# A Gated DeltaNet and chunk attention trunk: new planned durations, two yields, and the ends of the FFNs in another order

## The chip, the core and the metric

The kernel runs on one core of one Trainium2 chip. A core has five instruction queues, each in order: PE (TensorE, matmuls and transposes, with PEld as its weight load), DVE (VectorE), ACT (ScalarE), POOL (GpSimd) and SP (SyncE, which only issues DMAs). The engines meet through semaphores; data lies in SBUF (128 partitions) and PSUM (where matmuls add up). The metric is device microseconds (us) of one execution.

## What is computed

The input is a sequence of 1024 rows of width 1024 in float32. Layer 0 is a gated DeltaNet (8 heads of 128, chunks of 64) and a convolutional FFN of width 2816; layer 1 is softmax attention over bands of chunks and such an FFN; a last RMSNorm follows.

```python
def gated_deltanet(xn, w_in, conv_w, A_log, dt_bias, out_norm_w, w_out):
    proj = xn @ w_in
    qkv = jax.nn.silu(causal_dwconv(proj[..., :A_CONV_WIDTH], conv_w))
    z = proj[..., A_CONV_WIDTH:A_CONV_WIDTH + A_V_WIDTH]
    ...
    o = chunk_gated_delta_rule(q, k, v, beta, g)
    o = rmsnorm(o, out_norm_w) * jax.nn.silu(z.reshape(bsz, seq, A_HEADS, A_HEAD_V))
    return o.reshape(bsz, seq, A_V_WIDTH) @ w_out

# in chunk_gated_delta_rule, for each chunk of 64 rows
    v_new = u_c - w_c @ state
    o_c = qd @ state + a_c @ v_new
    state = state * dec + ke.T @ v_new

def conv_ffn(xn, w_up, conv_w, conv_b, w_down):
    h = causal_dwconv(xn @ w_up, conv_w) + conv_b
    gate, val = h[..., :FFN_DIM], h[..., FFN_DIM:]
    return (jax.nn.silu(gate) * val) @ w_down

def trunk(h):                       # the loop over layers, written out
    h = h + gated_deltanet(rmsnorm(h, a_norm[0]), ...)
    h = h + conv_ffn(rmsnorm(h, f_norm[0]), ...)
    h = h + chunk_attention(rmsnorm(h, b_norm[0]), ..., kv)
    h = h + conv_ffn(rmsnorm(h, f_norm[1]), ...)
    return rmsnorm(h, final_norm)
```

## The kernel before

**Precision.** Each float32 operand of a matmul is split into a high and a low part of a shorter type: ACT casts the high part (`whi` of a weight, L102; `uh`, `eh`, `dh`, L1444; `fh`, L1854), and POOL or DVE subtracts it from the original for the low part (`wlo`, L104; `ul`, `el`, `fl`, all on the helper line L1423). A product is then three matmuls (high by high, high by low, low by high). A moving operand has 512 columns.

**Stages.** The trace shows, in order: the prologue (norm of x and its transposes, until about 60 us), the delta stage (60 to 680), the first FFN (until about 1300), attention and the second FFN (its last stretch from 2455 on), and the last norm. In the delta stage the projections, the delta rule and the out projection are woven together.

**The delta stage's planner.** The order of PE, DVE and ACT is written by `Flow` (from L199): it keeps a planned time `T`, a planned "free from" time for D (DVE), A (ACT) and G (POOL), and a list of jobs (Python generators) with ranks. `wv.on("D", cost)` books `cost` us on an engine and returns when it is done; `yield t` gives the turn back until planned time `t`; `later` does so for a function. Between the jobs PE gets dense matmuls (of a projection's or the out projection's weight tile). Costs change no instruction, only which one is issued next. POOL and SP take their instructions in an order that the framework's scheduler sets. Two lines carry the planner's core:

```python
self.free[e] = max(self.free[e], self.T + 0.2, after if e != "G" else 0.0) + cost + 0.05
return max(self.free[e], after + cost) + 0.1
```

Its jobs that the change touches:

- `split_tile` (L639) splits a weight tile of a projection: a cast on ACT, four pieces on POOL (L104).
- `project` (L667) does the short convolution on DVE (L682, L686) and SiLU by tanh (ACT L691, POOL L692 and L693); its `th` is one of a pair of 512-column buffers with the tag `zt`, which `yo`, `zt`, `ez` and `sq` share.
- `qnorm` (L716) transposes (PE L721) and takes sums of squares (ACT L725). `decay` (L750) makes the decay matrices. `gram` (L738) makes k k^T, scales it on DVE into `mn` (L790), and copies the diagonal blocks on POOL into `cm` (L795).
- `invert_blocks` (L851) inverts the 32x32 diagonal blocks on DVE column by column; `merge` (L890, PE L911 to L952) builds larger inverses from them.
- `chain` (L978) is the recurrence over chunks: PE L992 (w by state), DVE L994, PE L996 (`U`), ACT `y` L1001, PE L1005, and DVE L1011, which updates the state S.
- `finish` (L1019) normalises outputs: squares on ACT, an inverse square root by integer tricks and Newton steps on tiny DVE tiles (`rsqrt`, L607 to L612, into `rr`), and a scaling of `vv` on POOL (L1041). Then `turn` (L1047, PE L1051, into PSUM `po`) for all but the last heads, whose results go to DRAM and come back in `yz` (L1105) with their gates, or `turn_last` (L1091, PE L1098). `split_yt` (L1122) splits the result for the out projection, whose tiles (`out_tile`, L1306, PE `acco`) go over the first half of the sequence (s = 0) and then over the second (s = 1).
- `begin_input` (L1225) loads the first two weight tiles and x, and runs transposes and the first products.

`gg`, which holds log decays, is read for the last time by the cumulative sums in the prologue (L1206).

**The FFN.** Width 2816 is 22 tiles j of 128 channels. The up product of a tile (gate and value, 2 x 1024 columns) is computed by a Strassen scheme of seven products, in the order 1, 7, 6, 5, 2, 4, 3; each is 12 matmuls into a PSUM bank. Products 2, 4 and 3 add into the banks of 1, 7 and 5. After product 6 the tile's `keep` and `keep7` are made on DVE from the banks of 6 and 7 (two operations named `keep`, L1423), after 5, 4 and 3 the other parts of the result (`vpre`, `gpre`). `left_sum(j, n)` prepares the weight sum r of product n on DVE; `operand(j, n)` splits it. The convolution is three taps each (`taps`, DVE L1551, ACT L1548), then `silu` (ACT L1554), `gated` (DVE, val x gate) and, for the last four tiles (18 to 21), `hidden` (ACT `hidh` L1568, DVE `hidl`). The others go through nine groups of Strassen down products, whose sums stand in DRAM: `send` and `send_e` add stages by accumulating DMAs that POOL issues (L1793, L1800). Tiles 18 to 21 are multiplied plainly in the end phase "f": `cut_last` (L1851) splits their down weights, and `part` (L1865, first FFN) or `tile_of` (L1939, second) run the matmuls for k = 0 to 3, one k a tile. Until now a first sweep over the column (or row) tiles takes k = 0 to 2, a second k = 3, for the first half; the other half has all four at once.

The order is by hand: `step` appends a PE step to a list `seq`, `pos` holds its place, and `at(i, f, rank)` puts other engines' work ahead of step i, by rank. `end` is the place of the last up product, `fin_at` that of the last down group's product 4.

**The last norm.** `norm_out` (L2325): ACT's Square with a sum (the last tile in two halves), a square root, DVE's reciprocal (L2347), then for each half a DVE operation with the scale and the gain `g_fin` (L2349) and a store on SP's queue (L2350).

## Time and profile before

| what | value |
|---|---|
| runs (3) | median 2588.57 us, 2588.05 to 2591.74 |
| the profiled execution, its own time | 2588.85 us |
| its span, first to last instruction | 2587.0 us |
| granted TensorE clock over the span | 0.996 |
| PE busy | 2506.2 us, 97% |
| DVE, POOL, ACT busy | 1861.0, 1476.3, 1414.3 us |
| DMA packets | 325.15 MB, mean 126 GB/s |

How to read the lines that follow. A timeline row has the start and the length in us, the engine, the line of the kernel, the operation, output<-inputs, partitions x elements and type, and how many instructions were joined (x2); in brackets stands how long the engine was idle before it, and what ended that. A row of waits has the engine, what it wanted to run, what released it, the total us, the number of waits and the longest. A row of groups has the count, busy us, mean ns of one, and the idle time before them. A row of windows has the window, its length, the busy us and count of PE, PEld, DVE, ACT and POOL, PE's granted clock as a share of full speed, the DMA engines' busy share and GB/s. PE's matmuls overlap: a row's 0.39 us is its passage, and the next starts 0.227 us later.

### The profile page before, as it was taken

The numbers are of one execution on the slowest core, as the hardware profiler recorded it, in microseconds if no ns is written. First come the engines' busy times: TensorE is split into PE (matmuls) and PEld (weight loads), VectorE is DVE, ScalarE is ACT, GpSimd is POOL, SyncE is SP. The second block draws the span as 40 slices with busy tenths as digits, with TensorE's granted clock in tenths as the row PEclk, the third lists the DMA queues.
The fourth block names the chain that finished last, engine by engine and source line by source line (L and its number), as shares of the span: only waits on it lengthen the run. The fifth ranks groups of instructions, "written<-read, shape, count | busy, mean of one in ns | idle before, by whom it ended". The sixth has DMA issues, their size and how long they took to land.

```text
span 2587.0 us, 39395 instructions
## 1 busy us (share of the span) xinstructions
PE 2506.2 (97%) x13933; PEld 2068.8 (80%) x13933; DVE 1861.0 (72%) x3102; ACT 1414.3 (55%) x2735; POOL 1476.3 (57%) x1466
## 2 busy tenths in 40 slices
PE   7999999999999999999999999999999999999988
PEld 5878788888877888888788888887876788888877
DVE  5765864554588888888876666666488788888875
ACT  6444455464455555655556555565455655565553
POOL 3655543345437777777726444443433777777770
PEclk9999999999999999999999999999999999999999
DMA  4534435555436777777841211113332576777785
GB/s 128 139 100 118 127 101 161 147 166 156 121 82 135 147 144 153 156 153 152 173 157 54 65 52 56 45 50 100 104 97 79 138 151 143 154 155 150 158 190 174
DMA packets 320598, 325.15 MB, mean 126 GB/s; under 512 B 32912, under 2 KB 244624, under 8 KB 320400
## 3 DMA queue, kind: packets, MB, share of 16 engines
q1 hardware_dynamic: 289584, 219.59, 29.0%
q0 software_dynamic: 25920, 94.38, 20.5%
q10 hardware_dynamic: 4896, 8.65, 1.0%
q8 instruction: 110, 1.80, 0.3%
q14 instruction: 88, 0.72, 0.1%
HBM read 179.89 MB, written 142.67 MB: 125 GB/s over the span
## 4 chain that ended last, share of the span: by engine, by line
PE 54%; DVE 6%; POOL 3%; issue 3%; ACT 2%; DMA 1%; DVEq 0%; ACTq 0%; POOLq 0%
PE pu L1458 8%; PE pu L1456 8%; PE pu L1457 8%; PE pd L1458 4%; PE pd L1457 4%; PE pd L1456 4%; PE acc L119 3%; PE acc L120 3%; PE acc L121 3%; PE ptp L2137 2%; POOL ul L1423 2%; PE sc L2109 1%; PE poT L2167 1%; PE poT L2166 1%; PE sc L2110 1%
## 5 line engine op out<-in xcount | busy, mean ns | idle before, releaser
L1423 POOL TENSOR_TENSOR ul<-r,uh 128x512 fp32r<-128x512 f32 x282 | 445.4, 1598 | 304.9 <-ACT uh L1444 280.9
L119 PE MATMUL acc<-xh,whi 128*128 128x512 f32 x896 | 375.4, 419 | 0.2
L120 PE MATMUL acc<-xl,whi 128*128 128x512 f32 x896 | 354.0, 395 | 2.0 <-POOL xl L421 1.0
L121 PE MATMUL acc<-xh,wlo 128*128 128x512 f32 x896 | 352.7, 394 | 0.0
L1444 ACT CAST uh<-r 128x512 fp32r<-128x512 f32 x296 | 181.7, 623 | 218.0 <-DVE r L1423 176.8
L104 POOL TENSOR_TENSOR wlo<-wraw,whi 128x256 fp32r<-128x256 f32 (+2 forms) x206 | 169.4, 851 | 159.1 <-ACT whi L102 139.3
L1456 PE MATMUL pu<-xh,uh 128*128 128x512 f32 x552 | 216.0, 391 | 2.8 <-ACT uh L1444 1.3
L1458 PE MATMUL pu<-xh,ul 128*128 128x512 f32 x552 | 215.7, 391 | 1.7 <-POOL ul L1423 1.7
L1457 PE MATMUL pu<-xl,uh 128*128 128x512 f32 x552 | 215.5, 390 | 1.0 <-POOL xl L421 1.0
L1778 ACT COPY stage<-pd 128x1024 f32<-128x1024 f32 x180 | 174.8, 1013 | 49.4 <-PE pd L1458 49.4
L121 PEld LDWEIGHTS acc<-xh,wlo 128*128 128x128 f32 x896 | 168.9, 189 | 37.3
L120 PEld LDWEIGHTS acc<-xl,whi 128*128 128x128 f32 x896 | 170.2, 190 | 25.5 <-DVE xl L1163 3.2
L119 PEld LDWEIGHTS acc<-xh,whi 128*128 128x128 f32 x896 | 169.9, 190 | 21.7 <-ACT xh L1162 1.1
L2117 POOL TENSOR_SCALAR sS<-sS,st 128x640 f32<-128x640 f32 (+4 forms) x128 | 85.3, 668 | 172.4 <-DVE st L2116 125.2
L1551 DVE SCALAR_TENSOR_TENSOR val<-vpre,colt,val 128x1023 f32<-128x1023 f32 (+2 forms) x92 | 152.8, 1661 | 38.6 <-ACT val L1548 38.4
L1423 POOL TENSOR_TENSOR dl<-a,dh 128x512 fp32r<-128x512 f32 x90 | 154.7, 1719 | 38.4 <-ACT dh L1444 38.4
L1551 DVE SCALAR_TENSOR_TENSOR gate<-gpre,colt,gate 128x1023 f32<-128x1023 f32 (+2 forms) x92 | 175.1, 1903 | 0.8
L1423 DVE TENSOR_TENSOR r<-r,r 128x512 f32<-128x512 f32 x168 | 131.8, 785 | 31.0 <-POOL ul L1423 29.6
L2115 ACT ACTIVATE sS<-sS,st 128x640 f32<-128x640 f32 (+4 forms) x128 | 89.3, 697 | 101.7 <-DVE st L2114 100.2
L1458 PEld LDWEIGHTS pu<-xh,ul 128*128 128x128 f32 x552 | 103.8, 188 | 26.0 <-POOL ul L1423 4.6
L1456 PEld LDWEIGHTS pu<-xh,uh 128*128 128x128 f32 x552 | 103.9, 188 | 25.3 <-ACT uh L1444 1.8
L1457 PEld LDWEIGHTS pu<-xl,uh 128*128 128x128 f32 x552 | 103.9, 188 | 23.5 <-POOL xl L421 2.1
(401 smaller groups left out, 7158.9 us busy)
## 6 DMA issues: line engine op xcount, KB each, us to landing
r<-in_f_w_up_dram SPq DMA_DIRECT2D x176, 256.0 KB, 4.3
d_r<-stage POOLq DMA_DIRECT2D x78, 512.0 KB, 7.8
d_c<-stage POOLq DMA_DIRECT2D x70, 512.0 KB, 8.1
a<-in_f_w_down_dram SPq DMA_DIRECT2D x72, 256.0 KB, 2.8
wraw<-in_a_w_in_dram SPq DMA_DIRECT2D x32, 512.0 KB, 4.7
d_e<-stage POOLq DMA_DIRECT2D x32, 512.0 KB, 8.9
wraw<-in_a_w_out_dram SPq DMA_DIRECT2D x16, 512.0 KB, 4.0
d_r<-h ACTq DMA_DIRECT2D x32, 256.0 KB, 3.8
```

Source lines behind the costliest of these rows:

```text
L104: nc.gpsimd.tensor_tensor(lo[:, c], raw[:, c], hi[:, c].bitcast(F32), op=ALU.subtract)
L119: mm(ps, hi[:, kw, wcol : wcol + P], rh[k][s], start=st, stop=False)
L120: mm(ps, hi[:, kw, wcol : wcol + P], rl[k][s], start=False, stop=False)
L121: mm(ps, lo[:, kw, wcol : wcol + P], rh[k][s], start=False, stop=sp)
L1423: tt = lambda eng, o, a, b, op: eng.tensor_tensor(o, a, b, op=op)
L1444: copy(hi, src)
L1456: mm(ps, w[0][:, cw], x[0], start=first, stop=False, skip_group_check=True)
L1457: mm(ps, w[0][:, cw], x[1], start=False, stop=False, skip_group_check=True)
L1458: mm(ps, w[1][:, cw], x[0], start=False, stop=last, skip_group_check=True)
L1551: nc.vector.scalar_tensor_tensor(t_[:, a:c1], p_[:, a - step : c1 - step], w[:, 2 - step : 3 - step], t_[:, a:c1], op0=ALU.mult, op1=ALU.add)
L1778: nc.scalar.copy(t_, ps)
L2115: nc.scalar.activation(S, S, AF.Exp, bias=st[:, 1:2], accum_out=st[:, 2:3])
```

## The change

The change has seven parts.

1. Planned durations are changed in `split_tile` (POOL is now booked, with 2.75), `decay`, `gram`, the scale's and `finish`'s rsqrt (1.2 to 3.5, 1.3 to 3.6), the columns of `invert_blocks`, the gate products, `split_yt` and `out_tile`.
2. `gram` yields ahead of POOL's copies into `cm`, and `finish` ahead of POOL's scalings of `vv`, until the DVE work that they read is through by the plan.
3. The tag `zt` has three buffers in the place of two; `soo` takes the place in memory of `gg`.
4. `yz` for the first half gets rank 1.5 in the place of 3.
5. `begin_input` splits the second weight after three steps of transposes.
6. The ends of both FFNs: r of tile 21's product 7 is prepared earlier; the last gate taps, SiLU and product of tile 20 come one step later; `hidden` of tiles 19 and 20 moves to product 5 of tile 21 and to the step after the last; the accumulating DMAs of `send_e` are issued by POOL behind more of its splits; the down weights' splits (`cut_last`) move; and the end phase's first half has three sweeps, with k = 0 and 1, then 2, then 3.
7. In the last norm's last tile the halves are multiplied by the gain ahead of the scale's arrival, and scaled one on DVE and one on ACT, whose queue also issues the second store.

```diff
@@ -612,7 +612,7 @@
-        soo, ff, rr = gt("soo"), gt("ff"), gt("rr")
+        soo, ff, rr = gg, gt("ff"), gt("rr")
@@ -638,7 +638,7 @@
-            wv.on("A", 1.0)
+            wv.on("G", 2.75, wv.on("A", 1.0))
@@ -687,7 +687,7 @@
-                    th = dp.tile([P, HALF], F32, name="th", tag="zt", bufs=2)
+                    th = dp.tile([P, HALF], F32, name="th", tag="zt", bufs=3)
@@ -750,12 +750,12 @@
-                yield wv.on("D", 0.75) - wv.slack
+                yield wv.on("D", 0.8) - wv.slack
...
-                yield wv.on("A", 1.4)
+                yield wv.on("A", 1.45)
@@ -785,10 +785,11 @@
-                wv.on("D", 1.4)
+                wv.on("D", 1.95)
...
-                slot[0] = t_ = wv.on("D", 1.3)
+                slot[0] = t_ = wv.on("D", 1.2)
+                yield t_ - wv.slack
@@ -799,7 +800,7 @@
-            wv.mark(("scale", t), wv.on("D", 1.2))
+            wv.mark(("scale", t), wv.on("D", 3.5))
@@ -877,7 +878,7 @@
-                t_ = wv.on("D", 0.3 + 3.1e-3 * i * i)
+                t_ = wv.on("D", 0.4 + 2.2e-3 * i * i)
@@ -1035,7 +1036,8 @@
-            t_ = wv.on("D", 1.3)
+            t_ = wv.on("D", 3.6)
+            yield t_ - wv.slack
@@ -1050,7 +1052,7 @@
-            yo = dp.tile([P, HALF], F32, name="yo", tag="zt", bufs=2)
+            yo = dp.tile([P, HALF], F32, name="yo", tag="zt", bufs=3)
@@ -1114,7 +1116,7 @@
-            yield wv.on("D", 0.7) - wv.slack
+            yield wv.on("D", 0.85) - wv.slack
@@ -1126,11 +1128,11 @@
-            wv.mark(("act", k, s), wv.on(e, 0.7 if e == "D" else 1.3, t))
+            wv.mark(("act", k, s), wv.on(e, 0.95 if e == "D" else 1.35, t))
...
-                zt = dp.tile([P, HALF], F32, name="zt", tag="zt", bufs=2)
+                zt = dp.tile([P, HALF], F32, name="zt", tag="zt", bufs=3)
@@ -1189,7 +1191,7 @@
-            ez = dp.tile([P, HALF], F32, name="ez", tag="zt", bufs=2)[:, 0:136].rearrange("p (c j) -> p c j", j=8)
+            ez = dp.tile([P, HALF], F32, name="ez", tag="zt", bufs=3)[:, 0:136].rearrange("p (c j) -> p c j", j=8)
@@ -1230,7 +1232,8 @@
-            wts = [load_w(a_w_in, m * P) for m in (8, 9)]
+            raws = [raw_tile(m * P) for m in (8, 9)]
+            wts = [split_w(raws[0], [P, KT, P])]
@@ -1240,6 +1243,8 @@
+                if s == 0:
+                    wts.append(split_w(raws[1], [P, KT, P]))
@@ -1274,7 +1279,7 @@
-        env["tmp"] = lambda: dp.tile([P, HALF], F32, name="sq", tag="zt", bufs=2)
+        env["tmp"] = lambda: dp.tile([P, HALF], F32, name="sq", tag="zt", bufs=3)
@@ -1328,7 +1333,7 @@
-                wv.on("D", 0.65, wv.on("A", 0.65))
+                wv.on("D", 0.75, wv.on("A", 0.65))
@@ -1337,7 +1342,7 @@
-            wv.later(wv.on("D", 0.6), then)
+            wv.later(wv.on("D", 0.7), then)
@@ -1385,7 +1390,7 @@
-                wv.add(3, ("yz", n % 6), wv.when(*[("gram", hd, 1) for hd in range(4, 8)]), yz(k, s))
+                wv.add(1.5 if s == 0 else 3, ("yz", n % 6), wv.when(*[("gram", hd, 1) for hd in range(4, 8)]), yz(k, s))
@@ -1648,6 +1653,8 @@
+                if j == FP - 1 and n == 1:
+                    at(i - 2, lambda j=j: left_sum(j, 7), 1.05)
@@ -1690,10 +1697,11 @@
-            when[j] = [(pos[j, 7], (v0, v1), 2), (nx(j, 1), (v2, g0), 2), (nx(j, 2), (g1,), 2)]
-            when[j] += [(nx(j, 3), (g2,), 2), (nx(j, 4), (silu,), 1.6), (nx(j, 5), (gated,), 2)]
+            late_ = 1 if j == FP - 2 else 0
+            when[j] = [(pos[j, 7], (v0, v1), 2), (nx(j, 1), (v2, g0), 2), (nx(j, 2 + late_), (g1,), 2)]
+            when[j] += [(nx(j, 3 + late_), (g2,), 2), (nx(j, 4 + late_), (silu,), 1.6), (nx(j, 5 + late_), (gated,), 2)]
             if j >= 2 * NG:
-                when[j].append(({18: fin_at + 5, 19: fin_at + 7}.get(j, nx(j, 6)), (hidden,), 1.9))
+                when[j].append(({18: fin_at + 5, 19: pos[FP - 1, 5], 20: end + 1}[j], (hidden,), 1.9))
@@ -1821,19 +1829,15 @@
-            for k, n in enumerate((6, 7, 4)):
-                at(i + 2 + k // 2, lambda u=u, n=n: send_e(u, n), 0.6)
+            for n, (k, r) in zip((6, 7, 4), ((2, 0.6), (2, 2.9), (3, 2.9)) if u == 0 else ((2, 2.9), (3, 2.9), (4, 2.9))):
+                at(i + k, lambda u=u, n=n: send_e(u, n), r)
...
-        last_at = [pos[FP - 1, s] for s in (3, 4, 5, 6)] + [end + 1] * 4
-        if layer == 1:
-            last_at = [pos[FP - 1, 2]] + last_at[:-1]
-            last_at[5] = end
-            last_at[7] = end + 2
+        last_at = [pos[FP - 1, s] for s in (3, 4, 5, 6)] + ([end, end, end + 1, end + 1], [end + 1, end + 1, end + 3, end + 3])[layer]
@@ -1858,7 +1862,7 @@
-            at(last_at[q], lambda q=q: cut_last(q), 1.5)
+            at(last_at[q], lambda q=q: cut_last(q), 0.9 if layer == 0 else 1.5)
@@ -1889,10 +1893,9 @@
-            for m in range(KT):
-                step(("f", 0, m, 0), part(0, m, range(3)))
-            for m in range(KT):
-                step(("f", 0, m), part(0, m, range(3, 4)))
+            for i, ks in enumerate((range(2), range(2, 3), range(3, 4))):
+                for m in range(KT):
+                    step(("f", 0, m, i) if i < 2 else ("f", 0, m), part(0, m, ks))
@@ -1975,10 +1978,9 @@
-            for t in range(4):
-                step(("f", t, 0), tile_of(t, range(3)))
-            for t in range(4):
-                step(("f", t), tile_of(t, range(3, 4)))
+            for i, ks in enumerate((range(2), range(2, 3), range(3, 4))):
+                for t in range(4):
+                    step(("f", t, i) if i < 2 else ("f", t), tile_of(t, ks))
@@ -2338,13 +2340,21 @@
+                nc.vector.tensor_tensor(ht[:, 0:HALF], ht[:, 0:HALF], g_fin[0][:, 0:HALF], op=ALU.mult)
                 yield
-                nc.scalar.activation(jk[:, HALF:SEQ], ht[:, HALF:SEQ], AF.Square, accum_out=ss[:, 0:1])
+                nc.vector.tensor_tensor(jk[:, HALF:SEQ], ht[:, HALF:SEQ], g_fin[0][:, HALF:SEQ], op=ALU.mult)
+                nc.scalar.activation(jk[:, 0:HALF], ht[:, HALF:SEQ], AF.Square, accum_out=ss[:, 0:1])
...
+            if t == KT - 1:
+                nc.vector.tensor_scalar(ht[:, 0:HALF], ht[:, 0:HALF], ss[:, 1:2], None, op0=ALU.mult)
+                nc.scalar.activation(ht[:, HALF:SEQ], jk[:, HALF:SEQ], AF.Copy, scale=ss[:, 1:2])
+                for i, q in enumerate((nc.sync, nc.scalar)):
+                    q.dma_start(out=out[t * P : (t + 1) * P, hs(i)], in_=ht[:, hs(i)])
+                return
...

```

## What is predicted, and from what

> **What bounds the kernel now.** I read the page's busy times first, then busy times by stage, then the waits of PE inside the stages that the change reaches, and last the timeline around each wait.
>
> ```profile
> PE 2506.2 (97%) x13933; PEld 2068.8 (80%) x13933; DVE 1861.0 (72%) x3102; ACT 1414.3 (55%) x2735; POOL 1476.3 (57%) x1466
> ...
> 60.00:680.00 620.00, 600.62 (x4918) 504.48 (x4917) 365.86 (x959) 304.20 (x833) 312.80 (x419) 1.00 0.48 137
> 1230.00:1300.00 70.00, 65.54 (x279) 52.81 (x278) 56.85 (x52) 35.89 (x53) 49.21 (x37) 0.98 0.83 185
> 2455.00:2545.00 90.00, 83.36 (x361) 66.52 (x361) 68.74 (x67) 41.95 (x61) 54.59 (x41) 0.96 0.90 220
> ```
>
> PE is busy for 97% of the span: the matmuls set the time, and the change neither adds nor removes one. It can only win or lose idle time of PE, and time in which PE runs at a lowered clock. The three window rows (length, then busy us of PE, PEld, DVE, ACT and POOL, PE's granted clock, share of DMA, GB/s) are the delta stage, and the ends of the first and the second FFN. Idle in them: 620 - 600.62 = 19.4 us, 70 - 65.54 = 4.5 us, 90 - 83.36 = 6.6 us. What the clock costs shows in short windows behind PE's gaps:
>
> ```profile
> 300.00:304.00 4.00, 3.91 (x15) 3.27 (x16) 3.56 (x5) 1.78 (x3) 4.00 (x7) 0.62 0.00 0
> 1289.60:1294.00 4.40, 4.40 (x13) 3.51 (x14) 3.73 (x4) 2.14 (x4) 2.72 (x2) 0.64 0.59 173
> 2520.30:2526.40 6.10, 6.10 (x15) 4.76 (x16) 6.10 (x6) 3.71 (x6) 4.36 (x3) 0.50 0.70 188
> ```
>
> PE is busy in all three at 0.62, 0.64 and 0.50 of its clock, so the work lost is 0.38 x 4.0 = 1.5, 0.36 x 4.4 = 1.6 and 0.50 x 6.1 = 3.05 us. I book these on the gaps just ahead of them.
>
> **The delta stage.** The new durations, the three-buffer tag, the rank of yz and the two new yields (`gram`, `finish`) act together: the planner writes another order of PE, DVE and ACT, and the same instructions run. Their worth is what PE waits for there:
>
> ```profile
> PE pq L721 <- POOL kq L693: 5.0, 3, 2.3
> PE pc L992 <- DVE S L1011: 3.6, 4, 2.3
> PE po L1051 <- POOL vv L1041: 2.5, 1, 2.5
> PE pm L911 <- DVE T L907: 1.8, 2, 1.3
> ...
> POOL vv L1041 <- DVE rr L612: 23.7, 7, 8.7
> ...
> 298.98 2.06 POOL L1041 TENSOR_TENSOR vv<-vv,rr 128x512 f32<-128x512 f32 x2 [8.69 <-DVE rr L612]
> ...
> 300.09 0.65 PE L1051 MATMUL po<-ident,vv 128*128 128x128 f32 x4 [2.54 <-POOL vv L1041]
> ...
> 578.22 1.15 DVE L608 TENSOR_SCALAR rr<-rr 128x8 int32<-128x8 int32 x1
> ...
> 583.00 0.17 DVE L612 SCALAR_TENSOR_TENSOR rr<-t,rr 128x8 f32<-128x8 f32 x1
> ...
> 596.21 2.82 POOL L104 TENSOR_TENSOR wlo<-wraw,whi 128x256 fp32r<-128x256 f32 x4 [2.73 <-ACT whi L102]
> ```
>
> The first four rows hold 5.0 + 3.6 + 2.5 + 1.8 = 12.9 us of the 19.4. The POOL row shows what `finish`'s yield is about: GpSimd stands 23.7 us in front of its scalings, 8.7 us at once, with whatever comes next in its queue (SiLU products, weight splits) behind them. Two rows further, that wait reaches PE: `po` starts 2.54 us late, and this gap is the one ahead of the 0.62 clock. The rsqrt behind it was planned at 1.3 us; from its first row shown to its last it takes 583.17 - 578.22 = 4.95 us here. A weight tile's split was planned at nothing on GpSimd and takes 2.82. With 3.6 and 2.75 the planner sees both, so a turn's transposes and a weight's first matmul stand later in PE's order and find their data ready.
>
> Which stalls vanish can't be read from the order alone, as a new order has new stalls. Bounds: every idle moment and the lowered clock gone, -20.9; idle doubled, +19.4. I take two thirds of the four rows and of the clock, (12.9 + 1.5) x 0.67 = -9.6, and give back 3.6, as much as the four waits on S, for stalls that the new order makes: **-6.0**. The new yields add no wait on an engine; they let the planner place other work ahead of GpSimd's scalings and copies. What stands behind them on GpSimd is then less held up. The turns move back in PE's order: the last one stood some 19 us of matmuls (at the 0.227 us a matmul that the FFN's row times below give) ahead of the out tiles that need it, and now 9; with less than that left over, PE stands at once, as in the 2.54 row.
>
> `soo` in the place of `gg` could add a wait for gg's last reader; that one is in the prologue's cumulative sums (L1206), ahead of every chain and `finish`: nothing. **The first weights** cost nothing either way: ACT still casts both in a row and GpSimd splits all eight pieces in the same place, in the order that the changed kernel is built with. Were the second split to move behind transposes, GpSimd alone would feel it; no matmul of that weight comes sooner.
>
> **The sends ahead of the FFN ends.** One of GpSimd's accumulating DMAs in each FFN (L1800) goes from ahead of operand splits to behind them.
>
> ```profile
> 1234.73 1.53 POOL L1800 DMA_DIRECT2D d_r<-stage  x1
> ...
> 1235.35 2.24 POOL L1423 TENSOR_TENSOR ul<-r,uh 128x512 fp32r<-128x512 f32 x1
> 1235.46 3.93 DVE L1423 TENSOR_TENSOR r<-r,r 128x512 f32<-128x512 f32 x1 [2.09 <-POOL ul L1423]
> ...
> 1239.31 0.68 DVE L1423 TENSOR_TENSOR val<-val 128x512 f32<-128x512 f32 x1
> ...
> 1241.61 0.49 PE L1456 MATMUL pd<-eh,dh 128*128 128x512 f32 x1 [0.86 <-ACT stage L1778]
> ```
>
> DVE's r takes 3.93 us beside GpSimd's splits, where the same operation takes 0.68 alone; ACT's eviction follows late, and PE loses 0.86. Without the send in front, the split starts 1235.35 - 1234.73 = 0.62 us sooner and all of this moves with it: -0.6 in each FFN (the second has the same order), **-1.2** in all, between 0 and -1.7.
>
> **First FFN's end.**
>
> ```profile
> 1283.34 0.39 PE L1456 MATMUL pu<-xh,uh 128*128 128x512 f32 x1
> 1283.59 2.31 DVE L1423 TENSOR_TENSOR hidl<-val,hidh 128x1024 fp32r<-128x1024 f32 x1
> 1285.82 2.29 DVE L1551 SCALAR_TENSOR_TENSOR gate<-gpre,colt,gate 128x1022 f32<-128x1022 f32 x1
> 1285.83 0.39 PE L1458 MATMUL pu<-xh,ul 128*128 128x512 f32 x1
> 1288.03 1.41 DVE L1423 TENSOR_TENSOR keep<-pu,keep 128x512 f32<-128x512 f32 x2
> 1289.58 0.47 PE L1456 MATMUL pu<-xt4h,uh 128*128 128x512 f32 x1 [3.36 <-DVE keep L1423]
> ```
>
> PE waits 3.36 us for the two `keep`s, which read the banks of products 6 and 7; product 4 (xt4h) adds into the latter. Both products were over before product 5, and that before product 2 began (1283.34); the keeps only stand behind hidl of tile 19 and a gate tap, 2.31 + 2.29 = 4.6 us. The change moves both behind them. The keeps then end near 1288.03 + 1.41 - 4.6 = 1284.8, ahead of product 2's end at 1285.83 + 0.23 = 1286.06. Gain 3.4, and 1.6 of clock: **-5.0**, at least -2. Late next are vpre, which frees product 3's bank, and that hidl. With r and gate in front vpre ends by 1284.8 + 0.7 + 2.3 + 0.7 = 1288.5; with fl too, hidl ends by 1288.5 + 1.4 + 2.3 = 1292.2, if GpSimd slows every one. A product takes 12 matmuls, 2.72 us (1283.34 to 1286.06; 0.227 each), so product 3 starts at 1288.8, the end phase at 1291.5, and that needs hidl behind three matmuls of tile 18 and two with hidh, at 1291.5 + 5 x 0.227 = 1292.6. Both just hold. Tile 20 is due only in the new second sweep of the end phase, after 48 matmuls or 10.9 us. The third sweep changes no count of matmuls.
>
> **Second FFN's end.**
>
> ```profile
> 2512.27 0.62 ACT L1444 CAST uh<-r 128x512 fp32r<-128x512 f32 x1 [4.88 <-DMA r<-in_f_w_up_dram]
> 2512.94 0.50 PE L1456 MATMUL pu<-xh,uh 128*128 128x512 f32 x1 [1.34 <-ACT uh L1444]
> 2514.30 0.50 PE L1458 MATMUL pu<-xh,ul 128*128 128x512 f32 x1 [0.62 <-POOL ul L1423]
> 2514.39 2.19 DVE L1423 TENSOR_TENSOR hidl<-val,hidh 128x1024 fp32r<-128x1024 f32 x1 [3.66 <-ACT hidh L1568]
> 2516.50 2.29 DVE L1551 SCALAR_TENSOR_TENSOR gate<-gpre,colt,gate 128x1022 f32<-128x1022 f32 x1
> 2518.72 1.41 DVE L1423 TENSOR_TENSOR keep<-pu,keep 128x512 f32<-128x512 f32 x2
> 2520.27 0.77 PE L1456 MATMUL pu<-xt4h,uh 128*128 128x512 f32 x1 [3.38 <-DVE keep L1423]
> ...
> q0 software_dynamic: 1109, 4.04, 77.3%
> ...
> r<-in_f_w_up_dram SPq DMA_DIRECT2D x1, 256.0 KB, 16.0
> ```
>
> Here 1.34 + 0.62 + 3.38 us are idle and 3.05 go to the clock: 8.4. Keep again stands behind hidl and gate. But a weight load r lands 16.0 us after its issue while GpSimd's queue q0 holds the DMA engines 77.3% of the time (2483 to 2511), and in the new order ACT's cast of a down weight (fh) stands behind the cast of that r, and DVE's fl, another gate and the keeps behind fh. With r as late as now: fh until 2512.9 + 0.6, fl 0.7, gate 1.3, keeps 1.4, so 2516.9 against product 2's end at 2516.7. The gap shrinks from 3.4 to about 0.3 and the clock stays up: -3.1 - 3.05. Of the other 1.96 I take 0.85, as the sends start later and leave q0 open a little, and give 0.5 back for vpre, which with r and gate in front ends at up to 2520.6 where product 3 wants it at 2519.7: **-6.5**, between -3 and -8.4.
>
> **The last scaling.**
>
> ```profile
> 2581.19 0.63 ACT L2342 ACTIVATE jk<-ht 128x512 f32<-128x512 f32 x1 [2.17 <-DVE ht L1423]
> ...
> 2582.47 1.42 DVE L2349 SCALAR_TENSOR_TENSOR ht<-ht,ss,g_fin 128x512 f32<-128x512 f32 x2
> ```
>
> Two halves in a row on DVE, 1.42 us, become one on DVE beside one on ACT, near the Square's 0.63: 0.8 less for the second store, which gets ACT's queue. No store from that queue shows here; I take **-0.7**, between -0.8 and +0.5. The product with g_fin hides beside the Square.
>
> **Sum.** -6.0 - 1.2 - 5.0 - 6.5 - 0.7 = -19.4. The profiled execution took 2588.85 us (span 2587.0), 0.28 above the median of the runs: 2569.45 by its own time, **2569.2** as a median.
>
> **Rivals.** (1) The new order is no better: the waits of the delta stage go to other places. For it: 12.9 us in ten waits are 2% of the stage, any order may have them. The other parts alone give 2588.57 - 13.4 = 2575.2. (2) r comes later still, as q0's sends now reach further, and all of product 2 and the keeps with it: -3 there, 2572.7. Against it: the sends' bytes are the same. (3) The lowered clock isn't the gaps': it comes anyway, elsewhere, and the sum loses its 1.0 + 1.6 + 3.05 = 5.65 us: 2574.8. Against it: all three drops stand right behind a gap. The Trainium skill ("TensorE: Matmul & The Clock Gate", section "What's actually happening") has the clock fall after an idle window of 3413 ns; by that rule these gaps, of 2.54, 3.36 and 3.38 us, are too short to lower it, which is this rival; the trace doesn't agree, with 0.62, 0.64 and 0.50 behind them.
> (4) Slower: the chain.
>
> ```profile
> L1011 DVE SCALAR_TENSOR_TENSOR S<-S,dec,pc 128x128 f32<-128x128 f32 x32 | 11.0, 343 | 17.6 <-PE pc L1005 17.5
> ```
>
> Each of these 32 updates releases PE's next chain step; four are late now, at 3.6 / 4 = 0.9 us. If the new order puts DVE's longer work (4.95 us of rsqrt) ahead of most, the delta stage loses 0.9 for each; the other parts' 13.4 are eaten at 15 late updates, and 0.2% (5.2 us, about what tells a difference from none) is passed at 21. With 30: 2588.57 + 27 - 13.4 = 2602.2. Against it: PE has dense tiles to put between the steps, and the dearer durations space them wider.
>
> **How the numbers follow.** Forecast 0.50, (1) 0.18, (2) 0.10, (3) 0.04, (4) 0.13; 0.05 for 10 to 20 new chain stalls, which end within 0.2%. So faster 0.82, same 0.05, slower 0.13. The forecast's own bounds: all of the four waits and clock gone, the ends at their best, -14.4 - 1.7 - 5.0 - 8.4 - 0.8 = -30.3, 2558; nothing in the delta stage, 2575. The range reaches further down, for part of the other idle time there (up to -20.9, 2552), and up to some 14 late updates: 2555 to 2587.
>
> **What would show it.** Right: no PE wait on keep in either FFN end and clock 1.00 behind; GpSimd's wait on rr far under 23.7; PE idle in the delta stage near 13 us; the last two stores within 0.2 us of each other. Wrong: waits on S, U or turned tiles adding up to more than 19.4 us; r still landing after 2512 relative to the same product; a wait on hidl at the end phase's first tile.

## The result and the profile after

| | before | changed |
|---|---|---|
| first set of runs, median (range) | 2589.47 us (2588.05 to 2591.74, 4 runs) | 2574.11 us (2571.88 to 2575.93, 4 runs) |
| ratio, 95% interval | | 0.9939, 0.9922 to 0.9957 |
| second set, beside other kernels | 2590.74 us (9 runs) | 2570.84 us (5 runs), ratio 0.9924, 0.991 to 0.9939 |
| profiled execution: own time, span | 2588.85, 2587.0 us | 2572.95, 2571.2 us |

The change is a gain of 0.6 to 0.8%. Its forecast was 2569.2 us. As no matmul was added or removed, the span divides at PE's own milestones: the first matmul of each stage. (The changed kernel's lines lie a little lower in the file: L1461 to L1463 are the matmuls of L1456 to L1458, L1428 is the helper line L1423.)

| stretch | before | after | difference | forecast |
|---|---|---|---|---|
| start to the first FFN's first matmul | 679.88 | 667.36 | -12.5 | -6.0 |
| from there to its end phase | 616.83 | 612.71 | -4.1 | -5.6 |
| first FFN's end phase | 46.0 | 53.3 | **+7.3** | 0 |
| attention | 562.1 | 562.2 | +0.1 | 0 |
| second FFN to its end phase | 623.9 | 617.6 | -6.3 | -7.1 |
| to the end of the span | 58.3 | 58.0 | -0.3 | -0.7 |
| span | 2587.0 | 2571.2 | -15.8 | -19.4 |

The timeline rows of the kernel before that bound the first and third stretch (start, length, engine, line, what; the end phase's last matmul closes the third):

```profile
679.88 0.47 PE L1456 MATMUL pu<-xh,uh 128*128 128x512 f32 x1 [0.88 <-DVE h L1324]
...
1296.71 0.39 PE L1456 MATMUL pf<-hidh,fh 128*128 128x512 f32 x1
...
1342.72 0.39 PE L1458 MATMUL pf<-hidh,fl 128*128 128x512 f32 x1
```

And of the changed kernel, with what PE waits for inside the end phase:

```profile
667.36 0.47 PE L1461 MATMUL pu<-xh,uh 128*128 128x512 f32 x1 [0.87 <-DVE h L1329]
...
1280.07 0.39 PE L1461 MATMUL pf<-hidh,fh 128*128 128x512 f32 x1
...
1283.92 0.39 PE L1463 MATMUL pf<-hidh,fl 128*128 128x512 f32 x1
...
1285.44 0.69 DVE L1428 TENSOR_TENSOR gpre<-pu,keep 128x512 f32<-128x512 f32 x1
...
1286.28 0.47 PE L1461 MATMUL pf<-hidh,fh 128*128 128x512 f32 x1 [1.96 <-DVE gpre L1428]
...
1315.68 0.50 PE L1461 MATMUL pf<-hidh,fh 128*128 128x512 f32 x1 [0.58 <-DVE h L1428]
...
1321.67 1.39 PE L412 MATMUL pss<-ones,nacc 128*128 128x2 f32 x8 [1.58 <-DVE nacc L409]
...
1333.37 0.39 PE L1463 MATMUL pf<-hidh,fl 128*128 128x512 f32 x1
```

In its third stretch PE now stands three times, where before it stood only for `pss`, 0.6 us. Windows of the changed kernel (length, busy us of PE, PEld, DVE, ACT, POOL, PE's clock, DMA share, GB/s): the delta stage, then the stretches behind the gaps at the two `keep`s and behind that at `pss`.

```profile
60.00:680.00 620.00, 610.92 (x4981) 515.95 (x4980) 373.32 (x969) 310.76 (x843) 320.80 (x426) 1.00 0.48 140
...
1274.60:1280.00 5.40, 5.40 (x24) 4.50 (x25) 5.04 (x6) 4.40 (x7) 2.25 (x2) 1.00 0.72 210
...
1322.30:1328.40 6.10, 6.10 (x21) 5.23 (x22) 1.49 (x3) 0.90 (x2) 0.00 (x0) 0.50 0.12 43
2507.60:2512.00 4.40, 4.34 (x19) 3.62 (x20) 4.04 (x5) 3.80 (x6) 1.56 (x1) 1.00 1.09 365
```

PE's idle time in 60 to 680 us falls from 19.4 to 620 - 610.92 = 9.1 us. Behind both keeps the clock stays at 1.00. But behind `pss` it is 0.50 for 6.1 us: 3.05 us that the kernel before did not lose there.

What the lowered clock costs can be added up over a whole execution: in windows of 4 us, (1 - clock) x busy time of PE. That gives 7.2 us before and 7.4 us after, with a granted clock over the span of 0.996 in both. So the gain is idle time of PE, 80.8 us before and 66.6 us after; the lowered clock has moved to other places and not gone.

PE's waits in the delta stage after, and GpSimd's on rr:

```profile
PE pm L939 <- ACT X L932: 2.5, 1, 2.5
PE pq L721 <- POOL kq L693: 1.9, 2, 1.3
PE acc L119 <- DVE kq L686: 1.6, 1, 1.6
PE acc L121 <- POOL wlo L104: 1.1, 1, 1.1
...
PE pc L993 <- DVE S L1012: 0.4, 1, 0.4
...
POOL vv L1043 <- DVE rr L612: 31.9, 8, 9.2
```

Of the four rows that the sum was made of (12.9 us), 1.9 + 0.4 = 2.3 are left; new ones (2.5, 1.6, 1.1) are 5.2. GpSimd's own wait on rr rose, from 23.7 to 31.9, and PE has no row of waits on the `vv` behind it.

### The profile page after: what moved, and what is told of

The parts are those of the page before. It is cut to its first block, busy times and chain, and to the rows that moved or that the text cites. A ratio compares the mean times of both kernels' runs of the same rounds, so it can differ in the third digit from the quotient of the medians.

```text
span 2571.2 us, 39377 instructions
## 1 busy us (share of the span) xinstructions
PE 2504.6 (97%) x13933; PEld 2070.5 (81%) x13933; DVE 1863.4 (72%) x3103; ACT 1417.1 (55%) x2736; POOL 1471.5 (57%) x1466
## 3 DMA queue, kind: packets, MB, share of 16 engines
q0 software_dynamic: 25920, 94.38, 20.6%
## 4 chain that ended last, share of the span: by engine, by line
PE 54%; DVE 6%; issue 4%; POOL 3%; ACT 2%; DMA 1%; POOLq 0%; ACTq 0%; SPq 0%; DVEq 0%
PE pu L1463 8%; PE pu L1461 8%; PE pu L1462 8%; PE pd L1463 4%; PE pd L1461 4%; PE pd L1462 4%; PE acc L119 3%; PE acc L120 3%; PE acc L121 3%; POOL ul L1428 2%; PE ptp L2139 2%; PE sc L2111 1%; PE poT L2169 1%; PE poT L2168 1%; PE sc L2112 1%
## 5 line engine op out<-in xcount | busy, mean ns | idle before, releaser
L1428 POOL TENSOR_TENSOR ul<-r,uh 128x512 fp32r<-128x512 f32 x282 | 443.1, 1591 | 305.6 <-ACT uh L1449 290.0
L104 POOL TENSOR_TENSOR wlo<-wraw,whi 128x256 fp32r<-128x256 f32 (+2 forms) x206 | 170.2, 856 | 148.6 <-ACT whi L102 139.2
L1461 PE MATMUL pu<-xh,uh 128*128 128x512 f32 x552 | 215.4, 390 | 1.5 <-DVE h L1329 0.9
L1463 PE MATMUL pu<-xh,ul 128*128 128x512 f32 x552 | 215.4, 390 | 1.1 <-POOL ul L1428 1.0
L1428 POOL TENSOR_TENSOR dl<-a,dh 128x512 fp32r<-128x512 f32 x90 | 154.8, 1720 | 38.5 <-ACT dh L1449 37.2
L1428 DVE TENSOR_TENSOR r<-r,r 128x512 f32<-128x512 f32 x168 | 132.9, 791 | 29.4 <-POOL ul L1428 28.1
L1463 PEld LDWEIGHTS pu<-xh,ul 128*128 128x128 f32 x552 | 103.6, 188 | 24.6 <-POOL ul L1428 3.2
L1461 PEld LDWEIGHTS pu<-xh,uh 128*128 128x128 f32 x552 | 103.6, 188 | 23.5 <-issue 1.3
```

Source lines behind the costliest of these rows:

```text
L104: nc.gpsimd.tensor_tensor(lo[:, c], raw[:, c], hi[:, c].bitcast(F32), op=ALU.subtract)
L1428: tt = lambda eng, o, a, b, op: eng.tensor_tensor(o, a, b, op=op)
L1461: mm(ps, w[0][:, cw], x[0], start=first, stop=False, skip_group_check=True)
L1463: mm(ps, w[1][:, cw], x[0], start=False, stop=last, skip_group_check=True)
```

## The experiments

Twelve more runs were made, one of them of the changed kernel itself. The question was first where the delta stage's 12.5 us come from, as the change has four parts there, and then what lengthens the end phase. A kernel with one execution is read at the start of the first FFN, a single row; kernels that share an order of the delta stage show how firm that is: before and `ends` 679.9 and 682.0, the changed kernel three times (itself, `after_again`, `banks`) 667.4, 669.9 and 667.2. So one order alone moves by 2.1 to 2.7 us, and the delta stage's gain of 12.5 us is 10.0 with the repeat.

**Durations alone.** All changes of `wv.on` costs, nothing else.

```diff
-            wv.on("A", 1.0)
+            wv.on("G", 2.75, wv.on("A", 1.0))
...
-            t_ = wv.on("D", 1.3)
+            t_ = wv.on("D", 3.6)
```

> The kernel before with the changed planned durations alone (no new yields, two zt buffers, yz's old rank, old FFN ends). Measured against the first FFN's first matmul, which stands at 679.9 us before and at 667.4 with the whole change (-12.5). Theory: the durations carry the gain, so it starts at 668 to 672. Rival 'the yields carry it': 677 to 682. Rival 'any new plan differs by as much': anywhere in 667 to 692.

First FFN at 679.3 us; 2587.44 against 2588.83 us for the kernel before in one run each. The durations by themselves gain nothing that can be told from one execution.

**Yields alone.**

```diff
                 slot[0] = t_ = wv.on("D", 1.3)
+                yield t_ - wv.slack
                 cm = dq.tile([P, 4, 32], F32, name="cm", tag="cm", bufs=2)
...
             t_ = wv.on("D", 1.3)
+            yield t_ - wv.slack
             for hd, vv in zip(hds, vvs):
```

> The kernel before with the two yields alone. Theory (durations carry the gain): the first FFN starts at 676 to 682, within 4 us of before's 679.9. Rival 'the yields carry it': 667 to 671.

First FFN at 690.8 us, 10.9 later than before; 2599.87 us. GpSimd's wait on rr does fall in this kernel, from 23.7 to 11.5 us, so the yield does what it says, and the plan that comes of it is worse.

**A nudge of the plan before.** 

```diff
-                yield wv.on("D", 0.75) - wv.slack
+                yield wv.on("D", 0.8) - wv.slack
```

> The kernel before with one duration changed by 0.05 us (decay, 0.75 to 0.80): no better knowledge, but another plan from some 230 us on. It measures what a new plan does by itself. Theory: the start of the first FFN moves by less than 5 us from 679.9. Rival 'any new plan differs by as much': it moves by 8 us or more, either way.

First FFN at 692.3 us, 12.4 later, for 0.05 us in one number. The first waits of PE in this kernel's delta stage:

```profile
PE pc L992 <- DVE S L1011: 4.0, 4, 1.8
PE pm L911 <- DVE T L907: 3.6, 2, 3.2
PE pq L721 <- POOL kq L693: 3.4, 3, 2.3
```

They are of the same kinds as before's, at other places. Only 3.6 of the 12.4 us are more idle time of PE (23.0 us from 60 us to the first FFN, 19.4 before); the lowered clock takes 10.4 us there, where it took 1.7. So the theory that the durations carry the gain fell, and it was open whether the changed kernel was merely a lucky draw. Four kernels round it look into that.

**Two nudges of the changed plan.** (a) and (b):

```diff
-                t_ = wv.on("D", 0.4 + 2.2e-3 * i * i)
+                t_ = wv.on("D", 0.45 + 2.2e-3 * i * i)
...
-            wv.on("G", 2.75, wv.on("A", 1.0))
+            wv.on("G", 2.75, wv.on("A", 1.05))
```

> The changed kernel with one duration moved by 0.05 us (a column of the block inverse, 0.40 to 0.45). The first FFN starts at 667.4 us in the changed kernel, 679.9 before; one duration moved by 0.05 in the kernel before took it to 692.3. Theory 'luck of one plan': it starts 5 us or more away from 667.4, so at 672 to 690. Rival 'the four parts together make a better model, any plan from it is good': 664 to 671.

> A second draw of the same kind from the changed kernel: ACT's share of a weight split 1.00 to 1.05. Luck: the first FFN starts at 672 to 690. Better model: 664 to 671.

First FFN at 675.4 and 666.3 us (2579.65 and 2569.62 us). (a) met the range of luck, (b) that of the better model: there is a draw in it, and yet both are ahead of every plan with the old durations.

**Without the yields.** The two lines taken out of the changed kernel.

> The changed kernel without its two yields. Theory 'luck of one plan': the first FFN starts at 672 to 690, and so does any other edit of the plan. Rival 'costs and yields only work together': above 676, with waits of PE on tiles that GpSimd scales or copies (vv L1041, cm L795).

First FFN at 672.8 us (2577.04 us). That is 5.4 later than with them, and about all of it is clock: the lowered clock takes 6.8 us here and 1.5 in the changed kernel, while PE's idle time is 10.0 and 9.1 us. No gain of the yields in this plan shows. PE waits for no tile that GpSimd scales or copies, so the rival fell.

**Two zt buffers.** In the changed kernel:

```diff
-        soo, ff, rr = gg, gt("ff"), gt("rr")
+        soo, ff, rr = gt("soo"), gt("ff"), gt("rr")
...
-                    th = dp.tile([P, HALF], F32, name="th", tag="zt", bufs=3)
+                    th = dp.tile([P, HALF], F32, name="th", tag="zt", bufs=2)
```

> The changed kernel with two zt buffers (and soo in a place of its own). Luck: the first FFN starts at 672 to 690. Rival 'the third buffer is what lets the plan run': above 676, with waits on buffers of this tag (ACT's tanh or the turn's copy held up), and the jittered kernels stay at 664 to 671.

First FFN at 673.3 us (2578.89 us), and this difference is no draw of the plan: PE runs the very order of the changed kernel. One wait is new. ACT's tanh and PE's wait in the two-buffer kernel:

```profile
247.69 0.63 ACT L691 ACTIVATE th<-u 128x512 f32<-128x512 f32 x1 [5.74 <-DMA d_y<-yo]
...
PE pc L1006 <- ACT y L1002: 4.1, 2, 3.8
```

and the same tanh in the changed kernel:

```profile
241.86 0.62 ACT L691 ACTIVATE th<-u 128x512 f32<-128x512 f32 x1
```

With two buffers `th` has to wait until the DMA has stored a turn's `yo` out of the same pair; ACT stands 5.74 us, its `y` of the chain behind it, and PE 3.8 us for that. The difference is 673.35 - 667.36 = 6.0 us: 3.8 of waiting, 1.6 of a lowered clock right behind it (0.59 over 252 to 256 us), and a rest that one order's own spread covers. So the third buffer is worth at least 3.8 us in this plan.

**A second nudge of the plan before.** `finish`'s rsqrt at 1.4 in the place of 1.3.

> A second draw from the planner of before: the rsqrt in finish planned at 1.4 in the place of 1.3. Theory 'the old durations make worse plans on the whole, and the kernel before was a lucky one of them': the first FFN starts at 684 to 695. Rival 'before's neighbourhood is as good as the changed one's': below 680.

First FFN at 683.7 us (2593.88 us), 0.3 short of the theory's range and well above the rival's. All plans together, in us. Idle and clock are PE's idle time and what the lowered clock costs (by windows of 4 us), both from 60 us to the first FFN:

| kernel | first FFN | idle | clock |
|---|---|---|---|
| before; its order again (`ends`) | 679.9; 682.0 | 19.4; 19.1 | 1.7; 4.1 |
| old durations, second nudge | 683.7 | 21.0 | 2.8 |
| old durations, with yields | 690.8 | 26.5 | 5.8 |
| old durations, first nudge | 692.3 | 23.0 | 10.4 |
| new durations alone (`costs`) | 679.3 | 17.2 | 4.8 |
| changed without yields | 672.8 | 10.0 | 6.8 |
| changed with two buffers | 673.3 | 12.9 | 3.3 |
| changed, nudges (a) and (b) | 675.4; 666.3 | 13.9; 8.4 | 4.5; 1.3 |
| changed; once more | 667.4; 669.9 | 9.1; 8.8 | 1.5; 4.8 |

By the start, the means are 686.7 us with the old durations (four plans) and 672.4 with the new (six), and the nearest pair, 679.3 and 679.9, can't be told apart. The idle column is steadier: one order repeats within 0.6 us (8.4 in (b), 9.0 in the same plan with other banks below), and about half of what these kernels differ by from the one that they were made from is the clock. In it the step lies between `costs` (17.2) and the kernels that have all the other parts too, or all but one (8.4 to 13.9). So in the one plan that has them alone, the new durations don't bring it. The yields and the third buffer, each taken out alone, leave most of the step; the new rank of `yz`, which all those kernels share, was never tried alone, and no kernel has all the other parts with the old durations. What makes the better plans stays open among these.

**The ends alone.** The kernel before with parts 5, 6 and 7 of the change.

> The kernel before with the FFN ends, the first weights and the last scaling of the change, and the old delta stage. Theory: parts are independent, so the first FFN starts at 679.9 as before, its end phase takes 53.3 us in the place of 46.0, with a wait of about 2 us on gpre, and the whole is 3.4 us shorter than before. Rival 'the end phase's loss comes from what the new delta stage sends ahead': the end phase takes 46 us and the whole is 10 us shorter.

First FFN at 682.0 us, its end phase 50.7 us with the gpre wait of 1.94 us, 2584.43 us in all, 4.4 less than the kernel before beside it. So the end phase's loss belongs to the reordering and not to the new delta stage: in all nine profiles with the new ends it takes 50.6 to 53.3 us, the changed kernel's own profile being the longest, and 46.0 to 46.1 in those with the old ones. This kernel also shows PE's clock over a delta stage whose order it shares with the kernel before. Two windows of `ends`, where the clock is 0.60 and 0.50:

```profile
135.00:139.00 4.00, 4.00 (x14) 3.25 (x13) 3.72 (x14) 2.33 (x11) 1.25 (x4) 0.60 0.16 42
313.50:317.50 4.00, 4.00 (x12) 3.33 (x13) 1.04 (x2) 2.88 (x13) 3.80 (x9) 0.50 0.29 53
```

and the same windows of the kernel before, at 1.00 in both:

```profile
135.00:139.00 4.00, 4.00 (x20) 3.31 (x19) 3.75 (x13) 3.14 (x11) 1.57 (x5) 1.00 0.13 38
...
313.50:317.50 4.00, 4.00 (x20) 3.38 (x21) 2.95 (x5) 3.16 (x13) 3.79 (x8) 1.00 0.28 59
```

The gap ahead of the first window (PE waits for `kq`) is 2.3 us long in both kernels. Only this pair is a like one: the gap ahead of the second window is 3.2 us in `ends` and 1.5 in the kernel before. Another like pair stands in the changed kernel and in its repeat, behind the wait on X (`pm`) that ends near 549 us, 2.5 us long in the one and 2.7 in the other (the changed kernel first):

```profile
554.00:558.00 4.00, 4.00 (x45) 3.74 (x44) 3.69 (x9) 2.81 (x7) 0.00 (x0) 0.97 0.39 95
...
554.00:558.00 4.00, 4.00 (x27) 3.88 (x26) 2.90 (x6) 2.66 (x6) 0.24 (x1) 0.50 0.28 80
```

**Other banks for the end phase.** In the first FFN (the second half's first two column tiles take a double tile too):

```diff
-                        if s == 0 and m > 3:
+                        if m < (4, 2)[s]:
                             if m % 2 == 0:
                                 fps["d"] = pacc.tile([P, SEQ], F32, name="pf", tag="d", bufs=2)
...
-                    at(pos["f", s, m | 1 if s == 0 and m > 3 else m] + 1, closing(s, m), 0)
+                    at(pos["f", s, m | 1 if m < (4, 2)[s] else m] + 1, closing(s, m), 0)
```

> The changed kernel, but the first FFN's end phase takes the two free double PSUM tiles (tag d) for its first four column tiles and the four single banks (tag u) for the rest, so no matmul of the first sweep waits for gpre, which frees the last single bank. Theory: the three sweeps ask for the fourth bank after 18 matmuls in the place of 27, and that wait (2.1 us) and the lowered clock behind it or behind the next gap are the end phase's whole loss: it takes 46 to 47 us in the place of 50.7 to 53.3, no wait on gpre, and the kernel comes to 2566 to 2570. Rival 'DVE is late with the sums and the norm anyway': the end phase still takes 50 us or more, with waits on h and nacc.

2571.63 us (2570.34 to 2572.97, 5 runs), ratio to the kernel before 0.9927, 0.9915 to 0.9939: not to be told from the changed kernel, at 0.9924 beside it. The wait on gpre is gone, but the end phase still takes 1330.56 - 1279.96 = 50.6 us. The rival was right: what is saved early is lost at the norm's sum over the first half (`pss`), 3.0 us of waiting and about 1.5 of a lowered clock behind it. In the kernel with other banks:

```profile
1299.02 2.75 ACT L96 ACTIVATE wraw<-wraw,colt 128x128 f32<-128x128 f32 x9 [2.25 <-DMA wraw<-in_w_kv_dram]
1301.67 1.03 ACT L102 CAST whi<-wraw 128x1024 fp32r<-128x1024 f32 x1
1302.61 0.63 ACT L399 ACTIVATE nacc<-h 128x512 f32<-128x512 f32 x1
...
1303.79 1.94 DVE L401 TENSOR_TENSOR nacc<-nacc,nt 128x512 f32<-128x512 f32 x1 [3.90 <-ACT nt L399]
...
1310.13 2.47 DVE L401 TENSOR_TENSOR nacc<-nacc,nt 128x512 f32<-128x512 f32 x1 [0.20 <-ACT nt L399]
...
1320.44 0.27 PE L412 MATMUL pss<-ones,nacc 128*128 128x2 f32 x1 [3.04 <-DVE nacc L409]
```

and in the kernel before:

```profile
1315.19 2.16 ACT L96 ACTIVATE wraw<-wraw,colt 128x128 f32<-128x128 f32 x7 [2.29 <-DMA wraw<-in_w_kv_dram]
1317.26 0.62 ACT L399 ACTIVATE nacc<-h 128x512 f32<-128x512 f32 x1
...
1318.72 0.69 DVE L401 TENSOR_TENSOR nacc<-nacc,nt 128x512 f32<-128x512 f32 x1 [2.76 <-ACT nt L399]
...
1334.21 0.27 PE L412 MATMUL pss<-ones,nacc 128*128 128x2 f32 x1 [0.63 <-DVE nacc L409]
```

From the end phase's start, ACT's first square of the norm comes at 1317.26 - 1296.71 = 20.6 us before, and at 1302.61 - 1279.96 = 22.7 with the banks, as nine scalings and a cast of the next stage's weight (L96, L102) stand ahead of it in the place of seven. Two of DVE's sums take 1.9 and 2.5 us, each beside a GpSimd split of 2.4 us (L104, at 1302.78 and 1309.65), and the sum is ready at 40.5 us in the place of 37.5. Which of the two decides, and whether the three sweeps or the moved operations put the weight's work ahead, was not tried alone and stays open.

**The changed kernel again, and the best draw with the other banks** ((b)'s plan and the banks together).

> The changed kernel once more, as the neighbour of the others: 2572 to 2576. Its delta stage runs the same order as before, so the first FFN starts within 2 us of 667.4, the distance that two kernels with one order showed (679.9 and 682.0).

> The last draw of the plan that was good (first FFN at 666.3) together with the other banks: 2563 to 2567, if both gains add. If the plan's gain is lost between profile and plain runs: 2568 or more.

2570.84 us (2568.36 to 2575.23, 5 runs) and 2570.21 us (2567.88 to 2572.0, 4 runs; ratio 0.9921, 0.9907 to 0.9934). The repeat came 1.2 below its range. Of the combination, 666.6 us at the first FFN repeats (b)'s plan, but as the banks save nothing, it is no faster than the changed kernel. No version here beats it clearly.

## Why the prediction came out

The forecast was 2569.2 us; 2574.1 was measured (2570.8 in the repeat), faster and inside the range. That the sum is nearly right is in part luck: the delta stage gave 6.5 us more than its term, the end phase took 7.3 that had no term, and the gains of clock, 1.0 + 1.6 + 3.05 = 5.65 us, did not come in the balance. The three falls that they were taken from are gone, but others came, and over the span the lowered clock costs 7.4 us in the place of 7.2 (10.8 in the repeat). In that, rival (3), "it comes anyway, elsewhere", with 0.04, had it right; those read here do still stand behind gaps, only behind others.

- **Delta stage, -6.0: mis-sized, it was -12.5 (-10.0 in the repeat).** Of the rows named, 12.9 us became 2.3, and new ones came to 5.2 us, a little above the 3.6 given back. The 4.95 us of rsqrt were a long case: at 601.31 us the same operations take 2.0. Two thirds of the four rows was too little: PE's idle time fell by 10.3 us, to 9.1, where "near 13" was to show it, as other waits that had no term went too. The fall of clock behind `po` went, but one of 1.5 us came behind the wait on X. What the forecast lacked is that a plan is a draw: rival (1) came nearest, with 0.18, and plans with the old durations differ by up to 7 us of idle time. The reason given (rsqrt and the weight's split seen by the planner, so that data are ready) isn't shown: the durations alone leave 17.2 of the 19.4 us, taking the yields out changes the idle time by 0.9, and "GpSimd's wait on rr far under 23.7" was wrong, 31.9. "The three-buffer tag" was costed together with the rest; it holds at least 3.8 us by itself in this plan, through a buffer that a DMA was still reading, which no wait of PE in the kernel before showed.
- **Sends, half of the -1.2, and first FFN's end, -5.0: together -5.6 forecast, -4.1 measured.** The 0.86 us ahead of `pd` are gone, as foreseen. The gap at keep shrank to 0.94 us instead of none, and the clock stayed up. The step that was off is "the keeps then end near 1284.8": it took 4.6 us from DVE and left the durations of the rest. But the operation that DVE now has in front of the keeps lasts through three splits of GpSimd that follow one another; `ends` shows the same, with 5.25 us again. Which of the moves brings them together wasn't tried. The changed kernel:

```profile
1267.82 5.25 DVE L1556 SCALAR_TENSOR_TENSOR gate<-gpre,colt,gate 128x1023 f32<-128x1023 f32 x1
1267.92 1.59 POOL L1428 TENSOR_TENSOR ul<-r,uh 128x512 fp32r<-128x512 f32 x1
...
1269.18 1.56 POOL L1428 TENSOR_TENSOR fl<-fr,fh 128x512 fp32r<-128x512 f32 x1
...
1270.43 1.56 POOL L1428 TENSOR_TENSOR ul<-r,uh 128x512 fp32r<-128x512 f32 x1
...
1274.55 0.47 PE L1461 MATMUL pu<-xt4h,uh 128*128 128x512 f32 x1 [0.94 <-DVE keep L1428]
```

  A gate tap of 1.27 us (2504.92 below) takes 5.25 here. vpre and hidl "just hold", as was worked out: PE waits for neither.
- **The end phase, 0: the step that failed.** "The third sweep changes no count of matmuls" is true, and so is that tile 20 is ready; what it left out is banks and the work around, a loss that was put at nothing. Two k in the place of three in the first sweep ask for the fourth single bank after 18 matmuls, 4.1 us, and gpre frees it only 6.1 us in; and the norm's sums come later than PE. That is +4.7 in `ends`: 2.1 at gpre (1.94 of idle time and the last matmul's passage ahead of it), 1.6 of clock behind it, some 0.8 more at pss. It is +7.3 in the changed kernel's profile, where the clock fell behind pss instead and for longer, and +5.4 in its repeat. `banks` shows that the banks are not the whole of it: without the wait on gpre the phase still takes 50.6 us.
- **Second FFN, -0.6 and -6.5: -6.3 measured.** r landed earlier than assumed, 9.9 us after its issue and not 16.0, so no product waits for it, and rival (2) fell. That the later sends left q0 open isn't shown: q0 has 72.1% of the DMA engines' time from 2488 to 2499 us. But keep is late by 1.60 instead of 0.3, again through DVE's fl beside GpSimd:

```profile
2499.93 5.06 DVE L1428 TENSOR_TENSOR fl<-fr,fh 128x512 fp32r<-128x512 f32 x1 [1.29 <-ACT fh L1858]
2500.36 2.83 POOL L1428 TENSOR_TENSOR ul<-r,uh 128x512 fp32r<-128x512 f32 x2
...
2502.86 1.57 POOL L1428 TENSOR_TENSOR fl<-fr,fh 128x512 fp32r<-128x512 f32 x1
2504.92 1.27 DVE L1556 SCALAR_TENSOR_TENSOR gate<-gpre,colt,gate 128x1023 f32<-128x1023 f32 x1
...
2507.66 0.47 PE L1461 MATMUL pu<-xt4h,uh 128*128 128x512 f32 x1 [1.60 <-DVE keep L1428]
```

  The row of r's DMA in the changed kernel (2488 to 2499 us; KB, us from issue to landing):

```profile
r<-in_f_w_up_dram SPq DMA_DIRECT2D x1, 256.0 KB, 9.9
```

- **Last scaling, -0.7: -0.3.** The halves run side by side and the stores are issued 0.23 us apart (2567.45 and 2567.68), about as foreseen; the second then lands 2.5 us after its issue, where the last four stores before took 2.0.

```profile
2566.93 0.72 ACT L2354 ACTIVATE ht<-jk,ss 128x512 f32<-128x512 f32 x1 [0.23 <-DVE ss L2351]
2566.93 0.49 DVE L2353 TENSOR_SCALAR ht<-ht,ss 128x512 f32<-128x512 f32 x1
2567.45 0.33 SPq L2356 DMA_DIRECT2D out_dram<-ht  x1
2567.68 0.34 ACTq L2356 DMA_DIRECT2D out_dram<-ht  x1
```

- **First weights, 0.** The first FFN of `ends` starts no sooner than before, and the prologue's first product stands at 16.1 us before and after.
- **Rivals.** The chain, (4), did not come: waits on S fell to 0.4 us here. The nudged plans of before lost 3.8 and 12.4 us against it, but their waits on S, 4.7 and 4.0 us, are near the 3.6 there: a slower draw comes from all kinds of waits and from the clock, and not from the chain alone.

## What to carry to other kernels

Where a planner writes the order, its outcome is a draw: nudge one number by a hair several times on both sides before crediting a change, and compare groups. Compare their idle time, with what the lowered clock costs taken apart, as one order repeats the first within 0.6 us here, while the second differs by up to 3.3. Vary each part over the others' new state as well as over the old: here one part was never tried alone, and the cause stays open for that. When an operation is moved ahead at the end of a stage, count the banks and buffers that the following stage will ask for, by when, and not only its matmuls. And look which GpSimd operations stand in a row beside a VectorE operation that PE waits for: its length can be theirs.

## What the hardware showed

**PE's clock falls behind some gaps of 1.6 to 3.4 us, and in one execution and not in another.** The same 2.3 us gap at 135 us is followed by 1.00 in the kernel before and 0.60 in `ends`; behind 1.58 us and eight matmuls of two columns (pss) it fell to 0.50 in the changed kernel, and behind 1.60 us (the second keep) it did not. The Trainium skill ("TensorE: Matmul & The Clock Gate", section "What's actually happening") tells of a window of 3413 ns that runs freely; that fits a fall that depends on when the gap comes, but the runs show falls behind gaps less than half as long as the idle window that it names. The falls read here cost 1.5 to 4.8 us (the last is the repeat's behind X, where the changed kernel lost 1.5), so a gap's price is its length, or twice that and more. A change that closes some gaps needn't lower the sum: 7.2 us before, 7.4 after.

**A VectorE operation with two inputs in SBUF can wait through a whole row of GpSimd operations.** Two rows show it: 5.25 us for an operation that takes 1.27 at 2504.92, and 5.06 us for fl, whose shortest in the same kernel takes 0.68. They end about 1.1 and 0.6 us after the last of three GpSimd splits in a row. The Trainium skill ("SBUF — State Buffer", section "Who interferes with whom") gives the shared ports to whoever issues first, for the whole instruction, and has the other one blocked; here the VectorE rows start 0.10 and 0.43 us ahead of the first split, and VectorE was still blocked when the next GpSimd operations began.
